# A 8192 x 8192 float32 transpose on one core: when the stores are issued, in which order copies run, and a hinted loop branch

## The chip, the core and the metric

The kernel runs on one core of a Trainium2 chip. The core has TensorE (matrix multiply, here used to transpose blocks of 128 x 128), VectorE and ScalarE (element-wise work, here copies out of TensorE's result memory), GpSimd and SyncE, and 16 DMA engines that move data between the chip's main memory (HBM) and the on-chip memory. Each compute engine runs its own list of instructions in order and waits on semaphores. The metric is the device time of one execution in microseconds, as the median of several runs.

## The reference

```
def reference(x):            # x: 8192 x 8192 float32
    return np.transpose(x)
```

Nothing is computed except the transpose: 268.4 MB are read and 268.4 MB are written.

## The kernel before

The input is taken in 128 chunks, t = 0 to 127. A chunk is 128 rows of x by 4096 columns (2 MB); the first 64 chunks run down the left half of the columns, the next 64 down the right half (`chunks`, indexes s and c). `load(t)` at L103 brings chunk t into one of three input buffers `ins`; the first three loads are issued by SyncE, all later ones by ScalarE.

TensorE transposes a chunk in 32 pieces of 128 x 128 into its result memory, `pss[0]` for the first half (q = 0 to 3) and `pss[1]` for the second (q = 4 to 7). Every q has four pieces (`B`), and TensorE counts `s_pe` up after every second q, so four times a chunk (`NH`), at the 8th, 16th, 24th and 32nd transpose. The function `transposes(k)` begins with a wait on `s_ld[k]` for 18: 16 counts from the 16 DMA engines of the load, one from ScalarE and one from VectorE, which say that the copies of the chunk before are done and the result memory is free. TensorE's instructions form a loop, the "turns": a turn holds three chunks, the first turn two, and a compare-and-branch at the end goes back to the start of the body, 43 turns in all.

ScalarE (e = 0) and VectorE (e = 1) copy each half from the result memory into `regs`. This is nine regions of 2 MB in on-chip memory. Each of the eight q has an open "window" in one region, which gathers up to eight chunks, so that a store writes rows of up to 4 KB into the output. Each chunk closes one window: its region is stored to `out`, and the region becomes free when the store has landed (`s_st`). In the next chunk, that q opens a window in the region that has been free longest, so a chunk's copies may have to wait for the store of two chunks ago. Windows opened in chunk 0 are shorter, from one chunk (256 KB) to eight (2 MB); those that run over the border between the two halves of the columns are stored in two pieces; the last chunk closes all eight windows.

Copies that have the same spacing are merged into one instruction (`runs`): 1 to 4 copies per engine and chunk at L223. Before each the engine waits for the count of `s_pe` that it needs; the wait for the freed region stands ahead of all copies of that engine in the chunk. A copy that closes a window counts `s_cp[e]`; `store(q, e, count)` then lets ScalarE wait for that count and issue the store, in the middle of ScalarE's list, right after the copy if ScalarE did it. At the end of the chunk ScalarE waits for TensorE to have finished the chunk and issues `load(t + 3)`. All stores, and all loads but three, are in the one DMA queue of ScalarE, in the order in which ScalarE issues them: store t, load t+3, store t+1, load t+4. Store 0 is issued by the plain form (L168), all later ones by `wide_dma` (L28). SyncE waits at the end for every store.

Of the kernel before, what the change touches and what calls it, by code (L numbers as in the profile page):

```python
# [40 lines left out]
def kernel(  # L41
# [13 lines left out]
    nc = tc.nc  # L55
# [8 lines left out]
    NR = S // B  # L64
    NIN = 3
# [4 lines left out]
    with tc.tile_critical():  # L70
        nc.alloc_sbuf_tensor("pad", [P, 32], dt)
        ident = nc.alloc_sbuf_tensor("ident", [P, P], dt).ap()
        ins = [nc.alloc_sbuf_tensor(f"in{k}", [P, J], dt).ap() for k in range(NIN)]
        SIZE = B * W * P
        regs = nc.alloc_sbuf_tensor("regs", [P, NREG * SIZE], dt).ap()
        NH = NR // 2
        pss = [nc.alloc_psum_tensor(f"ps{k}", [P, NH * B * P], dt).ap() for k in range(2)]

        s_id = nc.alloc_semaphore("s_id")
        s_ld = [nc.alloc_semaphore(f"s_ld{k}") for k in range(NIN)]  # L80
        s_st = [nc.alloc_semaphore(f"s_st{k}") for k in range(NREG)]
        s_pe = nc.alloc_semaphore("s_pe")
        s_cp = [nc.alloc_semaphore("s_cpa"), nc.alloc_semaphore("s_cpv")]

        nc.gpsimd.memset(ident, 0.0).then_inc(s_id, 1)  # L85
        nc.gpsimd.wait_ge(s_id, 1)
        nc.gpsimd.affine_select(  # L87
            out=ident,
            in_=ident,
            compare_op=mybir.AluOpType.not_equal,  # L90
            fill=1.0,
            base=0,
            pattern=[[-1, P]],
            channel_multiplier=1,
        ).then_inc(s_id, 1)
        nc.vector.sem_inc(s_ld[0], 1)
        nc.scalar.sem_inc(s_ld[0], 1)

        chunks = [(s, c) for s in range(M // J) for c in range(CH)]

        def load(t):
            s, c = chunks[t]
            (nc.sync if t < NIN else nc.scalar).dma_start(  # L103
                out=ins[t % NIN], in_=x[c * P:(c + 1) * P, s * J:(s + 1) * J]
            ).then_inc(s_ld[t % NIN], 16)

        def transposes(k):
            nc.tensor.sem_inc(s_ld[k], -18).wait_op(s_ld[k], 18, "sem-ge")  # L113
            for q in range(NR):
                e, g = divmod(q, NH)
                for b in range(B):
                    tr = nc.tensor.transpose(  # L117
                        pss[e][:, (g * B + b) * P:(g * B + b + 1) * P],
                        ins[k][:, q * B * P + b:(q + 1) * B * P - B + b + 1:B],
                        ident,  # L120
                    )
                if q % 2:
                    tr.then_inc(s_pe, 1)

        T = len(chunks)
        assert T % NIN == NIN - 1
        pe = [nc.tensor.engine]
        nc.tensor.wait_ge(s_id, 2)

        turn = nc.alloc_registers("turn", engines=pe)  # L130
        nc.regs_mov(turn, 0)
        nc.br("turns", engines=pe)
        with nc.body("turns", valid_engines=pe):
            now = nc.snap(turn, min_val=0, max_val=T // NIN)
            with nc.tensor.If(now > 0):
                transposes(NIN - 1)
            for k in range(NIN - 1):
                transposes(k)
            nc.regs_alu(turn, turn, 1, op=mybir.AluOpType.add)
            nc.tensor.br_lt(turn, T // NIN + 1, on_true="turns", on_false="done")  # L140
        nc.switch_bb("done")

        for t in range(NIN):
            load(t)

        copied = [0, 0]
        free = list(range(NREG))
        stored = [0] * NREG
        window = {}

        def store(q, e, count):
            t0, r, parts = window.pop(q)
            nc.scalar.wait_ge(s_cp[e], count)
            base = 0
            pieces = []
            for s, a, z in parts:
                rows = (z - a) * P
                j0 = s * J + q * B * P
                dst = out[j0:j0 + B * P, a * P:a * P + rows]
                dst = dst.rearrange("(q b) i -> q b i", q=P)  # L160
                src = regs[:, r * SIZE + base:r * SIZE + base + B * rows]
                base += B * rows
                pieces.append((rows, dst, src))
            for rows, dst, src in sorted(pieces, key=lambda v: -v[0]):
                if any(stored):
                    st = wide_dma(nc, nc.scalar, "qActDynamicHW", dst, src)
                else:
                    st = nc.scalar.dma_start(  # L168
                        out=dst, in_=src.rearrange("q (b i) -> q b i", b=B)
                    )  # L170
                st.then_inc(s_st[r], 16)
                stored[r] += 1
            free.append(r)

        def closes(w, t):
            t0, r, parts = w
            return t + 1 == t0 + sum(z - a for _, a, z in parts)

        for t, (s, c) in enumerate(chunks):
            for e in range(2):  # L180
                eng = (nc.scalar, nc.vector)[e]
                go = s_ld[(t + 1) % NIN]

                place = []
                for q in range(e * NH, (e + 1) * NH):
                    if q not in window:

                        span = (q - c) % W + 1  # L190
                        r = free.pop(0)
                        parts = [(s, c, min(c + span, CH))]
                        if c + span > CH and t + span < T:
                            parts.append((s + 1, 0, c + span - CH))
                        window[q] = (t, r, parts)
                        if stored[r]:
                            eng.wait_ge(s_st[r], 16 * stored[r])
                    t0, r, parts = window[q]
                    k = [p[0] for p in parts].index(s)
                    base = r * SIZE + B * P * sum(z - a for _, a, z in parts[:k])  # L200
                    _, a, z = parts[k]
                    place.append((base + (c - a) * P, (z - a) * P))

                runs = []
                for g in range(NH):
                    if runs:
                        u = runs[-1]
                        gap = place[g][0] - place[g - 1][0]
                        if place[g][1] == place[u[0]][1] and abs(gap) < 2 ** 15 and (
                            len(u) == 1 or gap == place[u[1]][0] - place[u[0]][0]  # L210
                        ):
                            u.append(g)
                            continue
                    runs.append([g])
                for u in runs:
                    off, dist = place[u[0]]
                    gap = place[u[-1]][0] - place[u[-2]][0] if len(u) > 1 else 0
                    dims = [list(regs.ap[0]), [gap, len(u)], [dist, B], [1, P]]
                    o = bass.AP(regs.tensor, regs.offset + off, dims)
                    i = pss[e][:, u[0] * B * P:(u[-1] + 1) * B * P]  # L220
                    i = i.rearrange("p (l b i) -> p l b i", b=B, i=P)
                    eng.wait_ge(s_pe, t * NH + (e * NH + u[-1]) // 2 + 1)  # L222
                    cp = nc.scalar.copy(out=o, in_=i) if e == 0 else nc.vector.tensor_copy(out=o, in_=i)  # L223
                    ends = [e * NH + g for g in u if closes(window[e * NH + g], t)]
                    if ends:
                        cp.then_inc(s_cp[e], 1)
                        copied[e] += 1
                    if u is runs[-1]:
                        if ends:
                            eng.wait_ge(s_cp[e], copied[e])  # L230
                            eng.sem_inc(go, 1)
                        else:
                            cp.then_inc(go, 1)
                    for q in ends:
                        store(q, e, copied[e])
            if t + NIN < T:
                nc.scalar.wait_ge(s_pe, (t + 1) * NR // 2)
                load(t + NIN)
        for r in range(NREG):
            nc.sync.wait_ge(s_st[r], 16 * stored[r])  # L240

# [29 lines left out]
```

## Time and profile before

| | |
|---|---|
| median of 3 runs | 1262.03 us (1261.98 to 1262.59) |
| the profiled execution | 1262.98 us, span 1261.2 us |
| TensorE matmul | 741.5 us busy, 59% |
| TensorE weight load | 720.8 us, 57% |
| VectorE | 302.5 us, 24% |
| ScalarE | 252.8 us, 20% |
| moved by DMA | 536.97 MB, 426 GB/s mean over the span |
| mean granted TensorE clock | 0.751 |
| load, issue to landing | 21.7 us median (125 issues of ScalarE) |
| 2 MB store, issue to landing | 17.5 us median (114 issues) |

The span runs from the first to the last instruction of the execution that was profiled. PE is TensorE, PEld its weight load, DVE VectorE, ACT ScalarE, POOL GpSimd, SP SyncE. L117 is a line of the kernel. A row of the table by stretch gives, after the stretch and its length, the busy microseconds of PE, PEld, DVE, ACT and POOL with the number of instructions, then TensorE's granted clock, the mean busy share of the 16 DMA engines and the GB/s that they moved. In a row of the timeline stand start, length, engine, line and operation, and in brackets the idle time before it and what ended it. Apart from these views, the trace has a record of every DMA packet and, for every transfer, 16 landing counts, one for each DMA engine.

### The profile page before, as it was taken

The page shows a single profiled execution, that of the slowest core. Times are in us where ns is not written, and L with a number is a line of the kernel's source. Part 1 is how long each engine was busy: PE and PEld are TensorE (multiplying, and loading weights), DVE is VectorE, ACT ScalarE, POOL GpSimd, SP SyncE. Part 2 cuts the span into 40 slices and gives each one's busy share as a digit, 9 for nine tenths or more (in the row PEclk, how much of TensorE's full clock was granted, in tenths as well). Part 3 has the DMA queues.
Part 4 walks back from the last instruction along what each step waited for, and adds up shares of the span by engine and source line. Part 5 has one row for each costly group of instructions (what it writes and reads, how often), then busy time and mean ns, then how long its engine had stood idle before and what let it go on. Part 6 is the DMA issues. An engine that isn't in the chain of part 4 may idle for free. (4 is left out here: it accounts for less than half of the span.)

```text
span 1261.2 us, 9538 instructions
## 1 busy us (share of the span) xinstructions
PE 741.5 (59%) x4096; PEld 720.8 (57%) x4096; DVE 302.5 (24%) x250; ACT 252.8 (20%) x257; POOL 0.7 (0%) x6
## 2 busy tenths in 40 slices
PE   5665655656565655665566555656556555656561
PEld 5565655656565655665565555655556555655551
DVE  2322222222222222223222222222222222222220
ACT  3212121121111211122211221221111211121120
POOL 0000000000000000000000000000000000000000
PEclk9878677777868686777767777686777777686775
DMA  9999999999999999999999999999999999999998
GB/s 380 427 424 427 429 428 429 429 428 430 431 430 429 430 430 429 430 430 430 428 422 427 429 431 429 430 430 429 429 430 431 428 430 430 429 429 431 429 429 351
DMA packets 39273, 536.97 MB, mean 426 GB/s; under 512 B 4320, under 2 KB 4832, under 8 KB 6240
## 3 DMA queue, kind: packets, MB, share of 16 engines
q10 hardware_dynamic: 38832, 530.60, 98.9%
q1 hardware_dynamic: 432, 6.29, 1.2%
q14 instruction: 8, 0.07, 0.0%
q8 instruction: 1, 0.02, 0.0%
HBM read 268.44 MB, written 268.44 MB: 426 GB/s over the span
## 5 line engine op out<-in xcount | busy, mean ns | idle before, releaser
L117 PE MATMUL ps<-ident,in 128*128 128x128 f32 x4096 | 741.5, 363 | 492.6 <-PEq L113 492.6
L117 PEld LDWEIGHTS ps<-ident,in 128*128 128x128 f32 x4096 | 720.8, 220 | 513.0 <-issue 513.0
L223 DVE COPY regs<-ps 128x512 f32<-128x512 f32 (+3 forms) x250 | 302.5, 1246 | 933.1 <-PE ps L117 760.0
L223 ACT COPY regs<-ps 128x512 f32<-128x512 f32 (+3 forms) x256 | 251.5, 1015 | 980.5 <-PE ps L117 489.8
L223 ACT ACT_TABLE_LOAD x1 | 1.3, 1283 | 1.0 <-SPq L70 1.0
L87 POOL TENSOR_SCALAR_AFFINE_SELECT ident<-ident 128x128 f32<-128x128 f32 x1 | 0.3, 292 | 0.2 <-POOL ident L85 0.2
L85 POOL MEMSET ident<- 128x128 f32 x1 | 0.2, 204 | 0.5 <-SPq L70 0.5
L255 POOL MEMSET const-bfloat16-1.0<- 128x1 bf16 x1 | 0.1, 101 | 0.0
L255 POOL MEMSET const-uint8-127<- 128x1 uint8 x1 | 0.1, 101 | 0.0
L255 POOL MEMSET const-float32-0.0<- 128x1 f32 x1 | 0.1, 98 | 0.2 <-issue 0.2
L255 POOL MEMSET const-float32-1.0<- 128x1 f32 x1 | 0.1, 98 | 0.0
## 6 DMA issues: line engine op xcount, KB each, us to landing
in<-in_x_dram ACTq DMA_DIRECT2D x125, 2048.0 KB, 21.7
out_dram<-regs ACTq DMA_DIRECT2D x114, 2048.0 KB, 17.5
out_dram<-regs ACTq DMA_DIRECT2D x4, 1792.0 KB, 15.9
in<-in_x_dram SPq DMA_DIRECT2D x3, 2048.0 KB, 11.8
out_dram<-regs ACTq DMA_DIRECT2D x4, 1536.0 KB, 14.2
out_dram<-regs ACTq DMA_DIRECT2D x4, 1280.0 KB, 15.1
out_dram<-regs ACTq DMA_DIRECT2D x4, 1024.0 KB, 15.5
out_dram<-regs ACTq DMA_DIRECT2D x4, 768.0 KB, 17.8
```

What stands on the lines that cost most here:

```text
L85: nc.gpsimd.memset(ident, 0.0).then_inc(s_id, 1)
L87: nc.gpsimd.affine_select(out=ident, in_=ident, compare_op=mybir.AluOpType.not_equal, fill=1.0, base=0, pattern=[[-1, P]], channel_multipl ...
L117: tr = nc.tensor.transpose(pss[e][:, (g * B + b) * P:(g * B + b + 1) * P], ins[k][:, q * B * P + b:(q + 1) * B * P - B + b + 1:B], ident,)
L223: cp = nc.scalar.copy(out=o, in_=i) if e == 0 else nc.vector.tensor_copy(out=o, in_=i)
L255: nc = _bacc.Bacc("TRN2", target_bir_lowering=False, num_devices=1)
```

## The change

Five edits are made together.

1. `store` no longer waits for `s_cp`. For every chunk but the last, the stores of chunk t wait until `s_pe` shows the first count of chunk t+1. That count can't come before both engines have reported their copies of chunk t, since TensorE waits for these reports. The stores of a chunk are gathered in `closed` and issued by ScalarE after all of its copies of the chunk, and `load(t + 3)` follows them. In the last chunk stores still wait for `s_cp`, right after each copy.
2. The wait for a freed region moves from ahead of all copies to just ahead of the copy that writes into it, and that copy goes last among the engine's copies of the chunk.
3. Where there is such a copy, the first copy of the engine waits for the `s_pe` count that the engine's last copy needs, and waits for a count that was already seen are left out.
4. The last copy of an engine in a chunk reports to TensorE itself; the separate wait and increment after a copy that closed a window are gone. With 1 to 3 there are 129 semaphore instructions fewer.
5. In TensorE's loop, a hint location is marked at the start of each turn and the backward branch refers to it.

```diff
             now = nc.snap(turn, min_val=0, max_val=T // NIN)
+            hint = nc.tensor.mark_branch_hint_location()
...
-            nc.tensor.br_lt(turn, T // NIN + 1, on_true="turns", on_false="done")
+            nc.tensor.br_lt(
+                turn, T // NIN + 1, on_true="turns", on_false="done"
+            ).branch_hint(hint)
...
-        def store(q, e, count):
+        def store(q, e, t):
             t0, r, parts = window.pop(q)
-            nc.scalar.wait_ge(s_cp[e], count)
+            if t + 1 < T:
+                nc.scalar.wait_ge(s_pe, (t + 1) * NH + 1)
+            else:
+                nc.scalar.wait_ge(s_cp[e], copied[e])
...
                         if stored[r]:
-                            eng.wait_ge(s_st[r], 16 * stored[r])
+                            fresh[q - e * NH] = (s_st[r], 16 * stored[r])
...
+                runs = sorted(runs, key=lambda u: any(g in fresh for g in u))
+                seen = t * NH + e * NH // 2
                 for u in runs:
...
-                    eng.wait_ge(s_pe, t * NH + (e * NH + u[-1]) // 2 + 1)
+                    need = t * NH + (e * NH + u[-1]) // 2 + 1
+                    if u is runs[0] and len(runs) > 1 and any(g in fresh for g in runs[-1]):
+                        need = t * NH + (e * NH + max(v[-1] for v in runs)) // 2 + 1
+                    if need > seen:
+                        eng.wait_ge(s_pe, need)
+                        seen = need
+                    for sem, value in [fresh[g] for g in u if g in fresh]:
+                        eng.wait_ge(sem, value)
                     cp = nc.scalar.copy(out=o, in_=i) if e == 0 else nc.vector.tensor_copy(out=o, in_=i)
                     ends = [e * NH + g for g in u if closes(window[e * NH + g], t)]
-                    if ends:
+                    if t + 1 == T:
                         cp.then_inc(s_cp[e], 1)
                         copied[e] += 1
+                        for q in ends:
+                            store(q, e, t)
+                        continue
                     if u is runs[-1]:
-                        if ends:
-                            eng.wait_ge(s_cp[e], copied[e])
-                            eng.sem_inc(go, 1)
-                        else:
-                            cp.then_inc(go, 1)
-                    for q in ends:
-                        store(q, e, copied[e])
+                        cp.then_inc(go, 1)
+                    closed += [(q, e) for q in ends]
             if t + NIN < T:
-                nc.scalar.wait_ge(s_pe, (t + 1) * NR // 2)
+                if not closed:
+                    nc.scalar.wait_ge(s_pe, (t + 1) * NH)
+                for q, e in closed:
+                    store(q, e, t)
                 load(t + NIN)
+            elif t + 1 < T:
+                for q, e in closed:
+                    store(q, e, t)
```

More of the change, by code (lines that the diff above doesn't have):

```diff
@@ L179 @@
         for t, (s, c) in enumerate(chunks):
+            closed = []
             for e in range(2):
@@ L184 @@
                 place = []
+                fresh = {}
                 for q in range(e * NH, (e + 1) * NH):
```

## The prediction

> **What bounds the kernel now.** I read the page first: how busy each engine is, then the DMA rows, then the instruction groups.
>
> ```profile
> DMA  9999999999999999999999999999999999999998
> GB/s 380 427 424 427 429 428 429 429 428 430 431 430 429 430 430 429 430 430 430 428 422 427 429 431 429 430 430 429 429 430 431 428 430 430 429 429 431 429 429 351
> q14 instruction: 8, 0.07, 0.0%
> HBM read 268.44 MB, written 268.44 MB: 426 GB/s over the span
> L117 PE MATMUL ps<-ident,in 128*128 128x128 f32 x4096 | 741.5, 363 | 492.6 <-PEq L113 492.6
> L223 DVE COPY regs<-ps 128x512 f32<-128x512 f32 (+3 forms) x250 | 302.5, 1246 | 933.1 <-PE ps L117 760.0
> L223 ACT COPY regs<-ps 128x512 f32<-128x512 f32 (+3 forms) x256 | 251.5, 1015 | 980.5 <-PE ps L117 489.8
> ```
>
> The 16 DMA engines are busy from the first slice to the last, at 429 to 431 GB/s in the middle. Every byte must be read once and written once. TensorE idles 492.6 us behind L113, its wait for a chunk; VectorE and ScalarE idle over 930 us each. So the question for each edit is whether a DMA engine ever runs out of work because of it.
>
> The second view is the table by stretch (columns: busy us of each engine, granted clock, DMA share, GB/s).
>
> ```profile
> 50.00:620.00 570.00, 338.93 (x1856) 329.57 (x1856) 137.82 (x108) 113.24 (x111) 0.00 (x0) 0.75 1.01 429
> 690.00:1230.00 540.00, 325.02 (x1771) 316.15 (x1772) 129.02 (x89) 107.88 (x108) 0.00 (x0) 0.74 1.01 430
> 1249.00:1254.00 5.00, 0.00 (x0) 0.00 (x0) 0.00 (x0) 0.00 (x0) 0.00 (x0) 0.50 1.04 428
> 1254.00:1256.00 2.00, 0.00 (x0) 0.00 (x0) 0.00 (x0) 0.00 (x0) 0.00 (x0) 0.50 0.63 268
> ```
>
> Nothing is left to win in the middle; time can only be lost at the start and won or lost in the last 6 us. Third, the timeline of one chunk late in the run, and of the start.
>
> ```profile
> 1188.77 5.40 PE L117 MATMUL ps<-ident,in 128*128 128x128 f32 x32 [3.10 <-PEq L113]
> 1193.23 2.36 DVE L223 COPY regs<-ps 128x1024 f32<-128x1024 f32 x2 [6.31 <-PE ps L117]
> 1193.59 2.05 ACT L223 COPY regs<-ps 128x512 f32<-128x512 f32 x4 [7.78 <-DMA out_dram<-regs]
> 1195.76 0.56 ACTq L28 DMA_DIRECT2D out_dram<-regs  x1
> 1196.36 0.60 ACTq L103 DMA_DIRECT2D in<-in_x_dram  x1
> ```
>
> ```profile
> 0.94 1.32 SPq L103 DMA_DIRECT2D in<-in_x_dram  x3
> 11.09 0.65 ACTq L168 DMA_DIRECT2D out_dram<-regs  x1
> 13.88 2.48 DVE L223 COPY regs<-ps 128x512 f32<-128x512 f32 x4 [13.88 <-PE ps L117]
> 15.07 0.36 ACTq L103 DMA_DIRECT2D in<-in_x_dram  x1
> 16.52 4.08 PE L117 MATMUL ps<-ident,in 128*128 128x128 f32 x32 [1.48 <-PEq L113]
> 17.75 1.07 ACT L223 COPY regs<-ps 128x512 f32<-128x512 f32 x2 [4.41 <-PE ps L117]
> 22.30 4.11 PE L117 MATMUL ps<-ident,in 128*128 128x128 f32 x32 [1.71 <-PEq L113]
> ```
>
> In the late chunk TensorE starts 0.14 us after the last DMA engine counted the load (landing records). The next chunk starts at 1198.52, 9.75 us later: one 2 MB load plus one 2 MB store at 430 GB/s. At the start the store of chunk 0 and load 3 are issued at 11.09 and 15.07, while the three loads from SyncE still fill the engines: load 2 lands at 18.20, and no DMA engine waits.
>
> **The change part by part.**
>
> *Stores wait for TensorE's next chunk, steady state.* ScalarE's store of chunk t, and load t+3 behind it, move from the end of the copies to the first count of chunk t+1. In the late chunk that is from 1195.76 to about 1198.52 + 1.9 = 1200.4 (eight of 32 transposes, 5.4 to 6.2 us per chunk, plus the signal; chunk 127 starts at 1227.81 and its first copy at 1229.80), 4.7 us later. When load t+1 has landed everywhere, the slowest engine still holds store t-1 and load t+2, 9.76 us of work. The late store reaches the engines 0.14 + 2.0 + about 1.0 us after the landing (1.0: SyncE's first issue at 0.94, first packet at 1.97 in the packet records). Cover: 9.76 - 3.1 = 6.6 us. Cost 0. Before, the cover was some 11 us. The engine that is furthest ahead counts load 127 at 1222.77, the last at 1227.67; it runs 4.9 us ahead and keeps about 1.7 us of cover. If it ran dry, only its lead would shrink. If the slowest engine's cover went, every chunk would pay the excess, 125 times.
>
> *What is queued behind the new wait.* On ScalarE, the store, the load (0.56 and 0.60 us) and the copies of chunk t+1. ScalarE then starts copying about 3.2 us after TensorE's start instead of 2.0, and needs 2.05 us: done at 5.3, or at 6 where it waits for the older store (4.8 us after TensorE's start above). VectorE ends at about 6.8 (1195.59). Cost 0; TensorE's gap of 3.10 us covers it.
>
> *The same wait at the start.* Here it costs. Store 0 needs the first count of chunk 1, for which a ScalarE copy of before starts at 17.75. Load 2's last data is through at about 17.8. Store 0 then is issued at 17.75 instead of 11.09, its first packet comes at 18.8 if the queue answers as SyncE's did (1.03 us), and its 512 packets of 512 B (27 ns each on 16 engines, 0.86 us) end at 19.65; before, they ended at 18.25 (packet records). Load 3 and all behind it come 1.4 us late. Lower end: no latency, 18.6, +0.4. Upper end: the latency that store 0 showed before, 11.09 to its first packet at 14.9, 3.8 us: end 22.4, +4.2. I take 1.4, since SyncE's first issue also met an empty queue, while store 0 met one full of loads. Is there a second hole? Store 1 would be issued at 22.30 + 1.25 = 23.55 and arrive at 24.6, when load 3 ends (5.4 us after 19.65) at 25.0: none. Later: store 2 arrives at 30.4 against 31, store 3 at 36.2 against 38. After that the growing stores keep the queue full, so the 1.4 us is carried to the end.
>
> By the Trainium skill, page "DMA: Bandwidth & Descriptors", section "Latency and other measured facts", the first byte of such an issue comes after about 0.6 us. By that figure, taken as an estimate, the start would cost 1.0 us instead of 1.4; the row with 1.03 us decides here.
>
> *Copies into freed regions last, the first copy waits for all of its half.* On VectorE the first copy may start after TensorE's end, up to 1.3 us later (1184.40 against an end of 1185.67). Worst case: 6.67 us of TensorE at the 0.67 clock, 2.53 of VectorE and 0.2 of signals, 9.4 us against 9.76. Cost 0, cover 0.36 us; every 0.1 us above the cover would cost 0.1 us in each of the some 60 chunks that open a region on VectorE, 6 us.
>
> *129 semaphore instructions fewer.* At the 51 ns that L113's wait takes, 6.6 us in all, 0.05 us a chunk, on engines that idle over 7 us a chunk. 0. One refill of instructions less (8 packets of 8 KB in the body, up to 0.5 us on the engine it hits): between -0.5 and 0, taken as 0.
>
> *The hint.* 43 extra TensorE instructions, hidden in gaps of 3 us and more. Chunk 2 opens a turn and starts 0.15 us after VectorE's last copy ends (22.15), chunk 3 doesn't and also needs 0.15 us (27.96 to 28.11), so the branch costs nothing now and the hint can win nothing.
>
> *The tail.* Store 126 moves from 1225.65 to 1229.8 and arrives at 1230.9; the slowest engine has store 125 until 1232.5. The last eight stores wait for room in the queue (issues of 3 to 4 us between 1235 and 1249). The 256 KB store now goes behind the 2 MB one; the bytes are the same. 0, within 0.5 us either way.
>
> **Sum.** +1.4 us. The profiled execution took 1262.98 us (span 1261.2), so 1264.4 on its own base; it ran 0.95 us above the median of the runs, 1262.03, which gives **1263.4**. A difference of 0.2%, 2.5 us, is about what a measurement of this kernel can tell from no change.
>
> **Rivals.**
>
> *The hole at the start is wider (slower).* With the 3.8 us that store 0 took from issue to first packet, +4.2: 1266.2. For it: it is the only first issue on ScalarE's queue in the trace. Against: the engines were busy with loads then. It becomes slower than the bound from a latency of 2.1 us.
>
> *The hint fetches (slower).* If each of 43 turns fetched one 8 KB packet on one DMA engine (309 ns in the packet records), that engine loses 13.3 us. On the slowest engine: 1263.4 + 13.3 = 1276.7; on the one that is 4.6 us ahead at the end, 1272.1. Against: 8 instruction packets in all, so the loop stays on chip today.
>
> *The compute loop binds (slower).* Above 9.76 us for TensorE plus VectorE; 0.3 us over in 60 chunks gives 1263.4 + 18 = 1281. Against: 9.4 us at the lowest clock seen.
>
> *Late stores drain the queue in every chunk (slower).* From an arrival later than 9.76 us after the landing, 6.6 us above my estimate. One microsecond beyond costs 125 us: about 1388. The Trainium skill's "DMA: Bandwidth & Descriptors", section "Rules for kernel authors", asks to issue a DMA early and wait late, which this change does the other way round; the trace shows the two transfers queued ahead.
>
> *The DMA engines' lag shrinks (faster).* The slowest engine ends at 1259.5, the fastest at 1254.9. The lag grew from 0.6 us (chunk 1) to 3.4 by chunk 12 while no queue was empty. A new rhythm of issues and fewer blocked ones (4.76 us at 628) could avoid it: 1263.4 - 4.6 = 1258.8 with all of it gone, 1261.1 with half. Against: an engine with work queued has no reason to care when the next issue comes. It ends faster than the bound from 3.9 us.
>
> **How the numbers follow.** Forecast 60, wider hole 20, hint 5, compute 3, drained queue 3, less lag 9 in 100. Faster 0.09, same 0.60, slower 0.31. The range leaves out 20: the hint, the compute loop, the drained queue and the full loss of lag. Its low end is the lower bound of the start (1262.4) less half the lag, 1260.1; its high end the wider hole plus the 0.6 us between the runs shown, 1266.8.
>
> **What the profile after would show.** Store 0 issued at about 17.7 and about a microsecond of DMA share below 1 near 18; TensorE's starts 9.76 us apart and about 1.4 us later than before from chunk 7 on; issue to landing near 13 us for 2 MB stores and 17 for loads; blocked issues near 628 to 680 gone; 8 or fewer instruction packets. The prediction is wrong if the DMA share in the middle drops, if TensorE's starts after landing grow above 0.14 us, or if the end of the slowest engine moves by more than the start did.

## The result, and the profile after

The changed kernel takes 1264.65 us in the median of 18 runs (1261.87 to 1267.91), the kernel before 1262.51 us (1261.13 to 1263.39, also 18). The ratio is 1.0018, 95% interval 1.0011 to 1.0024: 1.4 to 3.0 us slower. 1263.4 had been predicted, with a range from 1260.1 to 1266.8. The runs also lie further apart than before, 6.0 us against 2.3.

The page of the changed kernel, the rows that were read first before:

```profile
DMA  9999999999999999999999999999999999999998
GB/s 361 418 430 427 430 429 431 428 429 430 429 429 429 429 431 429 429 430 425 429 422 427 429 431 430 426 431 429 428 429 429 428 427 428 428 431 427 430 428 371
q14 instruction: 6, 0.05, 0.0%
L117 PE MATMUL ps<-ident,in 128*128 128x128 f32 x4096 | 744.1, 365 | 491.5 <-PEq L113 491.5
in<-in_x_dram ACTq DMA_DIRECT2D x125, 2048.0 KB, 16.8
out_dram<-regs ACTq DMA_DIRECT2D x114, 2048.0 KB, 12.6
```

Nothing has changed in what bounds the kernel: the DMA engines are busy throughout, at 422 to 431 GB/s in the middle. The first slice has lost most, 361 GB/s against 380. The queue is shallower, as it must be when issues come later: a load lands 16.8 us after its issue instead of 21.7, a 2 MB store after 12.6 instead of 17.5.

The timeline of the changed kernel, its start, and one late chunk:

```profile
8.44 5.87 PE L117 MATMUL ps<-ident,in 128*128 128x128 f32 x32 [8.44 <-PEq L113]
16.01 4.11 PE L117 MATMUL ps<-ident,in 128*128 128x128 f32 x32 [1.71 <-PEq L113]
17.25 0.64 ACTq L174 DMA_DIRECT2D out_dram<-regs  x1
17.93 0.63 ACTq L103 DMA_DIRECT2D in<-in_x_dram  x1
18.61 2.05 ACT L240 COPY regs<-ps 128x512 f32<-128x512 f32 x4 [5.40 <-PE ps L117]
...
1190.24 5.52 PE L117 MATMUL ps<-ident,in 128*128 128x128 f32 x32 [4.46 <-PEq L113]
1192.22 0.55 ACTq L28 DMA_DIRECT2D out_dram<-regs  x1
1192.80 0.61 ACTq L103 DMA_DIRECT2D in<-in_x_dram  x1
1193.89 2.05 ACT L240 COPY regs<-ps 128x512 f32<-128x512 f32 x4 [7.98 <-PE ps L117]
1194.84 2.36 DVE L240 COPY regs<-ps 128x1024 f32<-128x1024 f32 x2 [7.62 <-PE ps L117]
```

Store 0 is now issued at 17.25 us, 1.24 us after TensorE starts chunk 1, and load 3 behind it at 17.93 instead of 15.07. In the late chunk store and load go out 2 us after TensorE's start, ahead of the copies, and the copies end 6.96 us after that start (1194.84 + 2.36 against 1190.24).

The table by stretch of the changed kernel (busy us of PE, PEld, DVE, ACT and POOL, clock, DMA share, GB/s):

```profile
17.00:18.00 1.00, 1.00 (x10) 1.00 (x10) 0.00 (x0) 0.00 (x0) 0.00 (x0) 1.00 0.05 16
18.00:19.00 1.00, 1.00 (x11) 1.00 (x10) 0.00 (x0) 0.39 (x1) 0.00 (x0) 1.00 0.46 140
690.00:1230.00 540.00, 326.48 (x1764) 317.64 (x1765) 128.68 (x89) 107.98 (x107) 0.00 (x0) 0.74 1.01 429
1254.00:1256.00 2.00, 0.00 (x0) 0.00 (x0) 0.00 (x0) 0.00 (x0) 0.00 (x0) 0.50 1.04 434
```

and of the kernel before, the same two microseconds:

```profile
17.00:18.00 1.00, 1.00 (x10) 1.00 (x10) 0.00 (x0) 0.25 (x1) 0.00 (x0) 1.00 0.78 273
18.00:19.00 1.00, 1.00 (x11) 1.00 (x11) 0.00 (x0) 0.82 (x2) 0.00 (x0) 1.00 1.51 604
```

Here is the hole: from 17 to 19 us the share of the DMA engines is 0.05 and 0.46, where before it was above 1 on average (packet records overlap, so a share can exceed 1). The packet records give its parts. The data of load 2 ends between 17.18 and 17.70 us, one engine after another. Store 0's first packet comes 1.30 us after the start of its issuing instruction, at 18.55. By the sum of the records each engine idles some 1.3 us between 17 and 24 us. The first sixteen 16 KB packets after the hole take 1.26 us in the median, where they took 0.61 us before, another 0.65 us. Together that is about 2.0 us; the ninth of 16 engines counts load 5 at 39.14 us, 2.02 us later than before.

### The profile page after: what moved, and what is told of

Its sections match the earlier page's. It is cut to its first block, busy times and chain, and to the rows that moved or that the text cites. A ratio compares the mean times of both kernels' runs of the same rounds, so it can differ in the third digit from the quotient of the medians.

```text
span 1262.7 us, 9398 instructions
## 1 busy us (share of the span) xinstructions
PE 744.1 (59%) x4096; PEld 723.5 (57%) x4096; DVE 302.1 (24%) x250; ACT 252.7 (20%) x257; POOL 0.7 (0%) x6
## 6 DMA issues: line engine op xcount, KB each, us to landing
in<-in_x_dram ACTq DMA_DIRECT2D x125, 2048.0 KB, 16.8
out_dram<-regs ACTq DMA_DIRECT2D x114, 2048.0 KB, 12.6
```

## The experiments

Theory A: the cost is the hole behind chunk 0, and what it pushes back. Rivals: B, every late store costs, all through the run; C and later H, the hint costs; D, the hint gains; E, the order of copies matters; F, late stores cost by slow packets, on top of the hole. All times are medians, ratios to the kernel before on the same chip. Each kernel has one profile, the changed kernel two. The runs with the old order are made from the changed kernel: waits for counts already seen stay left out of them, and with edit 1 alone the shorter report of edit 4 stays too.

**Late stores, but not in the first eight chunks.** In the changed kernel:

```diff
+        def late(t):
+            return t >= 8
...
-            if t + 1 < T:
+            if t + 1 < T and late(t):
                 nc.scalar.wait_ge(s_pe, (t + 1) * NH + 1)
```

(and for the first eight chunks the counts of `s_cp` and the early store as before).

> The changed kernel, but stores of chunks 0 to 7 (and the loads behind them) are issued as in the kernel before, right after the copy; late from chunk 8 on. Theory A (the cost is the hole at the start): no hole near 17 to 18.6 us, time within 0.6 us of before, 1262.0 to 1263.1. Theory B (late issues cost in every chunk, or the drained faster DMA engines slow the run): still some 2 us above before, 1264 to 1265. Theory C (the hint costs): also 1264 to 1265.

1263.19 us (11 runs) against 1262.14; ratio 1.0010, 1.0001 to 1.0019. These 1.05 us are more than the 0.6 that A had allowed, and less than B's 2. The DMA share at 17 to 19 us is 0.82 and 1.43: no hole. What is left, 1 us, was taken up again below.

**The hole alone.** The kernel before, where only store 0 is late (`late(t)` is `t < 1`, no hint, old order):

> The kernel before, but the store of chunk 0 alone waits for the first count of chunk 1; no other edit. Theory A: the hole of 1.3 us is there and nearly all of the cost with it, +1.3 to +2.1 us on before. Theory B and C: within 0.6 us of before, apart from the hole of one chunk.

1265.53 us; ratio 1.0027, 1.0018 to 1.0036, so 2.3 to 4.5 us, more than the 1.3 to 2.1 that A had expected. The table by stretch of this kernel:

```profile
17.00:18.00 1.00, 1.00 (x11) 1.00 (x10) 0.00 (x0) 0.00 (x0) 0.00 (x0) 1.00 0.11 33
18.00:19.00 1.00, 1.00 (x10) 1.00 (x10) 0.00 (x0) 0.00 (x0) 0.00 (x0) 1.00 0.02 8
19.00:21.00 2.00, 1.49 (x13) 1.30 (x11) 1.43 (x3) 1.07 (x2) 0.00 (x0) 1.00 1.04 258
```

The hole is deeper here than in the changed kernel: store 0 is issued at 17.64 instead of 17.25, its first packet comes at 18.95, and each engine idles some 2.0 us instead of 1.3. One late store of 127 is enough for a loss as large as that of the changed kernel, with all other stores early. B isn't needed for it; whether the late stores in the middle add to it is taken up below.

**A deeper hole.** The changed kernel, store 0 waiting for the fourth count:

```diff
-                nc.scalar.wait_ge(s_pe, (t + 1) * NH + 1)
+                nc.scalar.wait_ge(s_pe, (t + 1) * NH + (4 if t == 0 else 1))
```

> The changed kernel, but the store of chunk 0 waits for the fourth count of chunk 1 instead of the first, 24 transposes or 3.1 us later. Theory A: the hole grows from 1.3 to some 4.4 us and the time with it, +3.1 us on the changed kernel, +5.2 on before (1267.7). Theory B and C: no more than 0.6 us above the changed kernel, since only one chunk of 128 issues later.

1267.17 us (5 runs); ratio 1.0038, 1.0024 to 1.0052, so 3.0 to 6.6 us above before; 5.2 had been expected. The store is issued at 20.33, each engine idles some 4.4 us, and the DMA share is 0.01 from 17 to 18 us and 0.00 from there to 21:

```profile
18.00:19.00 1.00, 1.00 (x10) 1.00 (x10) 0.00 (x0) 0.00 (x0) 0.00 (x0) 1.00 0.00 0
19.00:21.00 2.00, 1.29 (x11) 1.10 (x10) 1.64 (x3) 0.00 (x0) 0.00 (x0) 1.00 0.00 0
```

A deeper hole costs more, as A has it, but in these medians not one for one. On the same chip the changed kernel without the hint (next run), with a hole of 1.3 us, took 1265.98: three microseconds more of hole made 1.2 us more of time, where A had 3.1. The intervals of the two losses overlap, so this size is rough; the total comes near 5.2 because the loss with the shallow hole is larger on this chip than the 2.1 us that A had added to. In the two profiles the ninth engine counts load 5 at 41.46 and 39.08, 2.4 us apart, and the last packets end 1.5 us apart: a part is won back on the way. What wins it back was not tested.

**The hint.** The changed kernel without it:

```diff
-            hint = nc.tensor.mark_branch_hint_location()
...
-            ).branch_hint(hint)
+            )
```

> The changed kernel without the hint on the branch. Theories A and B: as the changed kernel, 1264 to 1265, TensorE starting 0.14 us after each landing. Theory C: back to before, 1262.5. A 16 KB instruction packet near 20 us, which the kernel before has and the changed one hasn't, should come back if the hint removed it.

1265.98 us; ratio 1.0027, 1.0018 to 1.0036. C falls: without the hint the changed kernel is no faster. The 16 KB instruction packet is back, at 17.52 us. The kernel even stood above the first value of the changed kernel, which led to theory D. Four more runs shared the next chip.

> The kernel before with the hint on the branch and nothing else. Theory A (the hole at the start is the cost, the hint is worth nothing): within 0.5 us of before. Theory D (the hint takes away the 16 KB instruction packet at some 17 to 21 us, and with it some 1 us, which would explain why the changed kernel without the hint stood 1 to 1.5 us above the changed kernel): 0.5 to 1.5 us below before, and no such packet in the records before the end.

The kernel before with the hint alone: 1263.75 us against 1262.52; ratio 1.0011, 1.0002 to 1.0020. D falls. The 16 KB instruction packet, at 20.76 us in the kernel before, is indeed gone from there; in this run it stands at 1261.86, behind the last store. That wins nothing.

> The kernel before with edits 2 to 4 alone (copies into freed regions last, merged waits, fewer semaphore instructions); stores are issued right after the copy as before, no hint. Theory A: within 0.5 us of before. Theory E (the order of the copies makes the DMA engines or the compute loop later): above before by 0.5 us or more, TensorE starting later than 0.14 us after its landings.

Edits 2 to 4 alone: 1262.19 us; ratio 0.9999, 0.9990 to 1.0008. E falls; order, merged waits and fewer semaphore instructions are worth nothing measurable.

> The kernel before with edit 1 alone: all stores but the last chunk's wait for TensorE's next chunk; copies in the old order, no hint. Theory A: as the changed kernel without the hint, 2 to 3.8 us above before, and order makes no difference. Theory E: clearly below the changed kernel without the hint, some 1 us or more.

Edit 1 alone: 1265.21 us (10 runs); ratio 1.0025, 1.0015 to 1.0034, the same as the changed kernel without the hint on the chip before (1.0027). So the order is worth nothing measurable beside late stores either.

> The changed kernel unaltered, on the same chip as the three others. Theory A with a worthless hint: as the kernel with edit 1 alone. Theory D: 1 to 1.5 us below it. Median 1264 to 1265.3, spread of its runs some 4 us as before.

The changed kernel on this chip: 1267.32 us (1263.78 to 1271.94); ratio 1.0038, 1.0026 to 1.0050, more than the 1.0018 of its 18 runs. Its median is 0.5 us above the predicted range here: the size of the loss differs between these two sets of runs by more than either interval admits. It is also 2.1 us above edit 1 alone, where A had expected the same time. The hole doesn't explain this: in the profile of these runs each engine idles some 1.0 us, less than in the first one.

These profiles show a second thing. From 300 to 1200 us the kernel before has 16 packets of 16 KB, of some 22,700, that take over 0.65 us; the changed kernel has 188, and 294 in its second profile. They are spread over the run and take 36 and 52 us in sum beyond the usual 0.61 us a packet, 2.3 and 3.3 us for each of the 16 engines. That is theory F.

Late stores alone don't bring them, though. Edit 1 alone has 355 (in an execution 4.5 us above its median) and late from chunk 8 on has 225; but three other kernels with late stores all through have few: the changed kernel without the hint 45, the deeper hole 11, only chunk 0 early (below) 18. These three land chunks 30 to 120 as fast as before, 9.77 us apart, and the changed kernel takes 9.80 in both of its profiles, 1.7 and 2.0 us in all. What decides between few and many was not found. The last four runs put theory F against the hint (H) and against a second hole.

**Late from chunk 8 on, no hint.**

> The changed kernel without the hint, its stores of chunks 0 to 7 issued early as before, late from chunk 8 on. Theory F (late issues cost some 1 us in the middle of the run by slow packets, on top of the hole): 0.7 to 1.5 us above before, with 10 or more packets over 650 ns in most stretches of 100 us after 300 us. Theory H (what the late-from-8 kernel with the hint lost came from the hint): within 0.5 us of before.

1262.11 us (1260.73 to 1266.66) against 1262.52; ratio 1.0002, 0.9992 to 1.0012. Late stores in the middle cost nothing that the median shows, though the profile has 241 slow packets: its last engine's landings from chunk 30 to 120 are 9.793 us apart against 9.777 before, 1.4 us in all, and its last packet ends at 1259.68 against 1259.51. Two of the 11 runs are above 1266. F's 0.7 to 1.5 us is not borne out as a median.

**Later still.** The same with the third count of the next chunk instead of the first:

```diff
-                nc.scalar.wait_ge(s_pe, (t + 1) * NH + 1)
+                nc.scalar.wait_ge(s_pe, (t + 1) * NH + 3)
```

> As the run before it, but the late stores wait for the third count of the next chunk instead of the first, 16 transposes or some 3 us later; the slowest DMA engine keeps about 3.5 us of cover, the fastest none. Theory F with thin cover as the cause: more slow packets than at the first count, 1 to 4 us above it. Theory H, or cover without meaning as the prediction had it: no more than 0.5 us above it. TensorE's cycle should still hold: copies end some 8.5 us after its start against 9.76.

1318.3 us (5 runs); ratio 1.0443, 1.0429 to 1.0457: 56 us, where at most 4 had been expected. Its timeline around chunk 59 and its table by stretch:

```profile
585.16 5.56 PE L117 MATMUL ps<-ident,in 128*128 128x128 f32 x32 [4.16 <-PEq L113]
589.80 0.55 ACTq L28 DMA_DIRECT2D out_dram<-regs  x1
590.38 0.61 ACTq L103 DMA_DIRECT2D in<-in_x_dram  x1
590.76 2.36 DVE L240 COPY regs<-ps 128x1536 f32<-128x1536 f32 x2 [7.37 <-PE ps L117]
591.03 2.05 ACT L240 COPY regs<-ps 128x512 f32<-128x512 f32 x4 [7.75 <-PE ps L117]
596.04 2.38 PE L117 MATMUL ps<-ident,in 128*128 128x128 f32 x10 [5.32 <-PEq L113]
```

```profile
300.00:400.00 100.00, 59.69 (x310) 58.04 (x308) 23.37 (x17) 18.84 (x13) 0.00 (x0) 0.67 1.01 411
400.00:500.00 100.00, 59.34 (x320) 57.73 (x320) 23.57 (x20) 17.80 (x14) 0.00 (x0) 0.70 1.00 409
```

The copies end at 593.12, 2.9 us before TensorE's next start at 596.04, and that start still comes 0.13 us after the landing: the compute loop does not bind. The DMA share stays at 1.00 to 1.01 while the rate falls from 429 to about 410 GB/s, so in the records the loss isn't idle time but longer packets: 1952 of 21,610 take over 0.65 us, 636 us too long in sum, 39.8 us for each engine from 300 to 1200 us. They come in step with the issues: 1493 of them start between 5 and 7 us after the issue of the latest store, a fifth of the time between two stores. Chunks come 10.24 us apart instead of 9.78, 0.46 us more, and 120 chunks of that are 55 us. The Trainium skill, page "DMA: Bandwidth & Descriptors", section "Rules for kernel authors", says to issue a DMA early and wait on it late; this run shows what the other way costs once the margin is gone.

**Only chunk 0 early.** As the run before the last, `late(t)` is `t >= 1`:

> As the first run, but only chunk 0's store (and load 3) is issued early, all others late. Theory A (the hole behind chunk 0 is the cost of the start): as the first run within 0.5 us. If later stores of the ramp arrive too late as well (second hole): 0.5 to 2 us above the first run, and a DMA share below 1 between 20 and 45 us.

1263.34 us; ratio 1.0010, 1.0001 to 1.0019. Some loss remains, and the table by stretch says where:

```profile
21.00:23.00 2.00, 1.23 (x10) 1.26 (x11) 0.62 (x2) 0.00 (x0) 0.00 (x0) 1.00 0.93 393
23.00:28.00 5.00, 3.30 (x27) 3.14 (x27) 2.49 (x4) 2.05 (x4) 0.00 (x0) 1.00 0.83 305
```

With the first hole closed, load 3 is done sooner and store 1 comes too late for it: a second hole, behind chunk 1. The ninth engine counts load 3 at 23.48 us, and store 1's first packet comes at 24.27. In the changed kernel load 3 is counted at 25.46, after such an arrival, and its share from 23 to 28 us is 1.00: there the first hole had covered the second.

**The hint again.**

> The kernel before with the hint alone, a second time, on the chip of the three others. Theory H: again 0.5 to 1.5 us above before. If the hint is worth nothing, within 0.5 us of before, and the first value was spread.

1262.69 us against 1262.52; ratio 1.0019, 0.9997 to 1.0042, wide because three of 11 runs took 1266.1, 1270.7 and 1276.4 us. With the first value of 1.0011 the hint is no gain. Whether it costs some 1 us or now and then costs much stays open; no profile fell on one of the long runs.

## Why the prediction was right, point by point

**The start** was the right place, and the only term of the sum; it was mis-sized. 1.4 us had been summed, about 2.0 us measured in the profile. Two of its numbers for store 0 were off. It was issued at 17.25 instead of 17.75, because TensorE took 5.87 us for chunk 0 and not 6.55. The first packet came 1.30 us after the start of the issuing instruction, not the 1.03 of SyncE's first load; the four other kernels with a late first store have 1.29 to 1.31. The difference is the length of the instruction: the store's takes 0.64 us and the load's 0.37, and the first packet comes 0.66 us after the end of either. The 0.6 us of the Trainium skill, page "DMA: Bandwidth & Descriptors", section "Latency and other measured facts", is further off than the row when it is counted from the instruction's start, as the prediction did; counted from its end, the trace agrees, with 0.66. The 18.25 us at which the prediction has store 0 end before is 18.49 in the records for the last of its 512 packets. A term was missing altogether: the first packets after the hole are 0.65 us longer. 1.4 - 0.5 + 0.27 + 0.65 gives 1.8, and 1.6 with the later end of store 0; the rest of the 2.0 has no term.

**The rival of a wider hole** rested on the 3.85 us of store 0 in the kernel before. Store 0 of the run with only chunk 0 early, with loads queued as before, shows 3.86 again, and the other profiles with an early store 0 have 3.79 to 3.89; where the loads had run out, or had at most about 1 us of data left, it was 1.31 at most. So choosing SyncE's row as the nearer one was right.

**"The 1.4 us is carried to the end"** did not hold as a step in the profile of the changed kernel, though the end came out near it. The slowest engine counts load 7 1.9 us later than before, load 20 at the same time (181.35 against 181.31), load 127 1.5 us later; the median engine is 1.9, 1.7 and 3.3 us later. Without the hint, and with few slow packets, the slowest engine is 2.0, 2.3 and 1.6 us later, which is nearer to the step. In the kernel before, the slowest engine itself loses some 3 us up to chunk 12; the changed kernel loses less there, and more in the middle by slow packets. Half the rival of a shrinking lag was thus seen: the engines count load 127 over 2.95 us instead of 4.90. It did not win: the last engine sets the end, and it ends later than before.

**Steady state at no cost** held as a median in the run that tests it (1.0002 with the start left early); the 4.8 us of the changed kernel's second set of runs is not accounted for, though its profile has 2.0 us of it in slower landings between chunks 30 and 120. But the step behind it failed: a cover of 6.6 us, and a price only once the slowest engine is empty. By that reckoning 2.7 us more lateness (an issue 4.64 us after TensorE's start instead of 1.98) would have left 3.9 us and cost nothing; it cost 56 us. The rival of the drained queue was put at an arrival 6.6 us above the estimate, and its real edge is less than 2.7 us away. So the remark that an engine with work queued has no reason to care when the next issue comes does not hold here. The prediction was right about the time and lucky about the margin.

**The order of copies and the semaphore instructions** at 0: right, 0.9999. **The hint** at 0: no gain, as predicted; a small cost can't be excluded. There are 6 instruction packets instead of 8 in 43 turns, so the loop needs none of its own. The drop comes with the fewer semaphore instructions and not with the hint: edits 2 to 4 alone have 6, the hint alone 8. **The tail** at 0: right. Load 127 is counted 1.47 us later than before and the last packet ends 1.48 us later, at 1260.99, so the tail adds nothing. The faster engines do run dry there, about 1 us each between 1227 and 1240, and all engines now end within 1.2 us of one another instead of 4.6.

Also as foretold: store and load land after 12.6 and 16.8 us (13 and 17), TensorE starts 0.13 us after each landing, the blocked issues near 628 us are gone.

## What to carry to other kernels

Where DMA bounds a kernel, look for the moment at which its queue is shortest, most often the first chunks, and ask of each moved issue whether it still arrives before that queue is empty; the other 120 chunks say nothing about it. A hole costs its idle time and a restart, here 1.3 us and 0.65 us at the start; how much of that is left at the end differed between the runs. And a queue that isn't empty isn't safe for that: test a margin by making the issue later on purpose, since the DMA share can stay at 1.00 while the packets get longer.

## What the runs showed of the hardware that was not expected

- An issue that finds the DMA engines out of data, or within about 1 us of it, needs 1.29 to 1.31 us from the start of its instruction to its first packet, 0.66 us from the end of that instruction. The first sixteen 16 KB packets then take 1.1 to 1.3 us in the median instead of 0.61. Both hold in the six profiles of five kernels that have a hole behind chunk 0. An issue behind queued loads needed 3.8 to 3.9 us.
- A DMA share of 1.00 doesn't show that the engines lose nothing. With stores 2.7 us later, packets took longer in sum by 636 us in 900 us on 16 engines, at a share of 1.00, while by addition the slowest engine still had work for 3.9 us when a store arrived. An engine that needs its work queued some 3.85 us ahead would fit both numbers; this is a guess, and no run was made that shows it.
- TensorE took 5.3 to 6.7 us for the 32 transposes of chunk 0 in the 14 profiles. In the changed kernel this moves the first store and so the hole, which may be part of why its runs lie further apart; the range of 1.4 us is less than the 6 us of the runs, so it isn't all of it.
